# Strided attention on one core: keys and values loaded in thirds, two of them on ScalarE's DMA queue

## The chip, the cores and the metric

The kernel runs on one core of a Trainium2 chip. Its time is the device time of one execution in microseconds. The kernel before was run eight times: the median is 129.92 us, the lowest 129.73, the highest 130.17. One more execution was profiled; it took 129.81 us, and the profile covers a span of 127.7 us of it, from the first to the last instruction.

## What is computed

Q, K and V have the shape (8, 12, 1024, 64) in float32, and `stride` is 64. Every query of a head attends to the same 16 positions of that head, 0, 64, 128 and so on to 960:

```python
attend_positions = np.arange(0, seq, stride)            # 16 of 1024
scores  = einsum('bhqd,bhkd->bhqk', q, k[attend]) / sqrt(64)
weights = exp(scores - max(scores))
weights = weights / (sum(weights) + 1e-10)
result  = einsum('bhqk,bhkd->bhqd', weights, v[attend])
```

So all of Q (25.2 MB) is read and all of the result (25.2 MB) is written, but only one row in 64 of K and of V is used: 96 heads of 16 rows of 64 floats, 0.39 MB of each.

## The kernel before

The 96 heads are worked on in 24 groups of four (`HG = 4`, `NG = 24`); one group is 1 MB of Q and 1 MB of result. Two groups share one "chunk" of 128 key rows (`NC = 12` chunks: 2 groups x 4 heads x 16 positions = 128 partitions). `k_raw` and `v_raw` hold these chunks, 128 partitions by 12 by 64 floats. Each is filled by one DMA before (lines 100 and 102), made of 1,536 rows of 256 bytes.

For a group g the steps are: `load` (the DMA of 1 MB of Q into one of nine `qn` buffers), `cast` to bf16 on POOL (line 211), `transpose` in 32x32 blocks on DVE (215), `scores` on PE (222) with the exponential on ScalarE (233), `sums_mm` and `sums_rec` (242, 251, 255) for the reciprocals of the sums, `outputs` on PE (264), `normalize` on DVE, ScalarE and POOL (277, 278, 282), and `store` (1 MB, from one of eight `out_sb` buffers).

Keys are prepared for eight groups (four chunks) at a time. `key_rows(m)` is four ScalarE instructions (165) that spread the rows of `k_raw`; `keys(m)` is eight small PE matmuls (175) and two ScalarE copies (183) into `k_t`. For the values, one DVE cast turns all of `v_raw` into bf16 (`v_bf`, line 300). `value_rows(n)` takes six chunks at a time: two PE matmuls (192) and two DVE casts out of PSUM (196) into `v_rep`. `values(g)` on POOL (203) builds what `outputs` uses. `key_rows(0)`, `keys(0)` and `value_rows(0)` run ahead of the loop; `key_rows(1)` and `(2)` follow in iterations 1 and 5, `keys(1)` and `(2)` in iterations 2 and 6, and `value_rows(1)` in iteration 3.

The order of the work on each engine is the order of the code. All DMAs are issued by the SP engine, and their order is the code's too: K, the Q block of group 0, V, the Q blocks of groups 1 to 8, and then in each iteration `store(g)` and `load(g + 9)`. Q blocks 0 and 1 are read in 128 rows of 8 KB, the others in 32 rows of 32 KB (line 97). Both `_copy` (line 35 in the profile, for Q and the stores) and `dma_start` (lines 100 and 102) go to the SP queue:

```python
    nc.sync.dma_start(k_raw, _ap_with(K, kv_src))
    load(0)
    nc.sync.dma_start(v_raw, _ap_with(V, kv_src))
    for g in range(1, QBUFS):
        load(g)
```

Of the kernel before, what the change touches and what calls it, by code (L numbers as in the profile page):

```python
# [11 lines left out]
FP32 = mybir.dt.float32  # L12
# [7 lines left out]
def _ap_with(ap: bass.AP, new_ap, extra_offset: int = 0) -> bass.AP:  # L20
    return dataclasses.replace(
        ap, ap=[list(p) for p in new_ap], offset=ap.offset + extra_offset
    )
# [27 lines left out]
def kernel(  # L51
# [8 lines left out]
    nc = tc.nc  # L60

    B, H, S, D = Q.shape
# [3 lines left out]
    P = 128  # L66
    HG = 4
    NG = B * H // HG
    NC = NG // 2
    SD = S * D  # L70
# [14 lines left out]
    psum_s = ctx.enter_context(tc.tile_pool(name="psm", bufs=2, space=bass.MemoryType.PSUM))  # L85
# [4 lines left out]
    k_raw = const.tile([P, NC, D], FP32, name="k_raw")  # L90
    v_raw = const.tile([P, NC, D], FP32, name="v_raw")
    kv_src = [[stride * D, P], [2 * HG * SD, NC], [1, D]]
    qn = {}

    def load(g):
        qn[g] = qn_pool.tile([P, 32 * D], FP32, name="qn", tag="qn")
        n = P if g < 2 else 32
        _copy(nc, qn[g], _ap_with(Q, [[HG * SD // n, n], [1, HG * SD // n]], g * HG * SD))

    nc.sync.dma_start(k_raw, _ap_with(K, kv_src))  # L100
    load(0)
    nc.sync.dma_start(v_raw, _ap_with(V, kv_src))
    for g in range(1, QBUFS):
        load(g)

# [16 lines left out]
    for c in range(2):  # L122
        for a in range(2):
            for e in range(2):
                nc.gpsimd.tensor_copy(
                    out=perm_v[:, c, a, :, e], in_=id_v[:, c, :, a]
# [5 lines left out]
    for i in range(3):  # L132
# [7 lines left out]
        out=slot_i, in0=iota_p, scalar1=4, scalar2=3,  # L140
# [6 lines left out]
        out=s_sel, in0=col4, scalar1=slot_f, scalar2=None, op0=ALU.is_equal  # L147
# [10 lines left out]
    v_bf = const.tile([P, NC, D], BF16, name="v_bf")  # L158
    v_rep = const.tile([P, NC, 2, D], BF16, name="v_rep")


    def key_rows(m):
        kr = k_raw[:, 4 * m : 4 * m + 4].rearrange("p n (q f) -> p n f q", f=2)
        for h in range(4):
            nc.scalar.activation(  # L165
                out=k_m[:, 4 * m : 4 * m + 4, :, h], in_=kr,
                func=AF.Copy, scale=slot_m[:, h : h + 1],
            )

    def keys(m):  # L170
        for u in range(2):
            kp = psum_sc.tile([P, 2, 2, 2, 4 * NK], FP32, name="kp", tag="sc")
            for i in range(2):
                for f in range(2):
                    nc.tensor.matmul(  # L175
                        kp[:, i, :, f],
                        lhsT=k_m[:, 4 * m + 2 * u + i, f].rearrange("p h q -> p (h q)"),
                        rhs=perm_k.rearrange("p c a b k -> p c (a b k)"),
                        start=True, stop=True,
                    )  # L180
            g0 = 8 * m + 4 * u
            dst = k_t[:, g0 : g0 + 4]
            nc.scalar.copy(  # L183
                _ap_with(dst, [dst.ap[0], [KW, 8], [32, 4], [1, NK]], extra_offset=NK),
                kp.rearrange("p i c f (s k) -> p (i c f) s k", s=4),
            )


    def value_rows(n):
        for c in range(2):  # L190
            vp = psum_s.tile([P, NC // 2, D], FP32, name="vp", tag="sm")
            nc.tensor.matmul(
                vp, lhsT=perm_v[:, c].rearrange("p a b e k -> p (a b e k)"),
                rhs=v_bf[:, 6 * n : 6 * n + 6], start=True, stop=True,
            )
            nc.vector.tensor_copy(out=v_rep[:, 6 * n : 6 * n + 6, c], in_=vp)  # L196

    qb, qt, wt, vb, rec, out_sb, o_ps, sm_ps = {}, {}, {}, {}, {}, {}, {}, {}

# [1 line left out]
    def values(g):  # L201
        vb[g] = vb_pool.tile([P, 4, D], BF16, name="vb", tag="vb")
        nc.gpsimd.tensor_tensor(  # L203
            out=vb[g], in0=mask,
            in1=v_rep[:, g // 2, g % 2].unsqueeze(1).to_broadcast([P, 4, D]),
            op=ALU.mult,
        )

    def cast(g):
        qb[g] = qb_pool.tile([P, 32 * D], BF16, name="qb", tag="qb")  # L210
        nc.gpsimd.tensor_copy(out=qb[g], in_=qn[g])  # L211

    def transpose(g):
        qt[g] = qt_pool.tile([P, 32 * D], BF16, name="qt", tag="qt")
        nc.vector.transpose(qt[g].bitcast(I32), qb[g].bitcast(I32))  # L215

    def scores(g):
        sc = psum_sc.tile([P, 512], FP32, name="sc", tag="sc")
        q = qt[g]
        for e in range(2):  # L220
            for f in range(2):
                nc.tensor.matmul(  # L222
                    sc, lhsT=k_t[:, g, f, NK * (1 - e) : NK * (1 - e) + P],
                    rhs=_ap_with(
                        q, [q.ap[0], [D, 8], [16 * D, 2], [2, 32]],
                        extra_offset=8 * D * e + f,
                    ),
                    start=e + f == 0, stop=e + f == 2,
                )
        w = wt[g] = w_bufs[g % 3]  # L230
        for a in range(2):
            wa = w[64 * a : 64 * a + 64]
            nc.scalar.activation(  # L233
                out=_ap_with(wa, [wa.ap[0], [P, 8], [1, 2], [2, 32]], extra_offset=64 * a),
                in_=sc[64 * a : 64 * a + 64].rearrange("p (t x q) -> p t x q", t=8, x=2),
                func=AF.Exp, bias=0.0, scale=scale,
            )

    def sums_mm(g):
        sm = sm_ps[g] = psum_s.tile([P, 8, 32], FP32, name="sm", tag="sm")  # L240
        for q in range(4):
            nc.tensor.matmul(  # L242
                sm[32 * q : 32 * q + 32], lhsT=sel32,
                rhs=wt[g][:, :, 32 * q : 32 * q + 32],
                start=True, stop=True, tile_position=(0, 32 * q),
            )

    def sums_rec(g):
        sm = sm_ps[g]
        smt = rec_pool.tile([P, 8, 32], FP32, name="smt", tag="smt")  # L250
        nc.vector.transpose(  # L251
            smt.rearrange("p i r -> p (i r)"), sm.rearrange("p i r -> p (i r)")
        )
        rec[g] = rec_pool.tile([P, 8, 4], FP32, name="rec", tag="rec")
        nc.vector.reciprocal(rec[g], smt[:, :, 0:4])  # L255


    def outputs(g, c):
        if c == 0:
            out_sb[g] = out_pool.tile([P, 4, 8, D], FP32, name="out_sb", tag="out_sb")  # L260
        ps = psum_o.tile([P, 4, 4, D], FP32, name="o_ps", tag="o")
        o_ps[g, c] = ps
        for i in range(4):
            nc.tensor.matmul(  # L264
                ps[:, i].rearrange("p s d -> p (s d)"), lhsT=wt[g][:, 4 * c + i],
                rhs=vb[g].rearrange("p s d -> p (s d)"),
                start=True, stop=True,
            )

    def normalize(g, c):  # L270
        ps = o_ps[g, c]
        i0 = 4 * c
        n = 4 if c == 0 else 2
        part = lambda k, m: out_sb[g][:, :, k : k + m].rearrange("p s i d -> p i s d")
        fact = lambda k, m: rec[g][:, k : k + m].unsqueeze(3).to_broadcast([P, m, 4, D])
        if n < 4:
            nc.scalar.copy(part(i0 + n, 4 - n), ps[:, n:4])  # L277
        nc.vector.tensor_tensor(  # L278
            out=part(i0, n), in0=ps[:, 0:n], in1=fact(i0, n), op=ALU.mult
        )  # L280
        if n < 4:
            nc.gpsimd.tensor_tensor(  # L282
                out=part(i0 + n, 4 - n), in0=part(i0 + n, 4 - n),
                in1=fact(i0 + n, 4 - n), op=ALU.mult,
            )

    def store(g):
        o = out_sb[g]
        _copy(
            nc,  # L290
            _ap_with(out, [[16 * D, P], [2 * SD, 2], [1, 16 * D]], g * HG * SD),
            _ap_with(o, [o.ap[0], [1, 1], [1, 32 * D]]),
        )
# [3 lines left out]
    cast(1)  # L297
    transpose(0)
    keys(0)
    nc.vector.tensor_copy(out=v_bf, in_=v_raw)  # L300
    scores(0)
    transpose(1)
    value_rows(0)
    values(0)
    values(1)
# [3 lines left out]
    for g in range(NG):  # L309
        if g + 2 < NG:  # L310
            transpose(g + 2)
        if g + 1 < NG:
            scores(g + 1)
        outputs(g, 0)
        outputs(g, 1)
        if g + 1 < NG:
            sums_mm(g + 1)
        if g + 2 < NG:
            values(g + 2)
        if g + 3 < NG:  # L320
            cast(g + 3)
        normalize(g, 0)
        normalize(g, 1)
        if g + 1 < NG:
            sums_rec(g + 1)
        if g in (1, 5):
            key_rows(g // 4 + 1)
        if g in (2, 6):
            keys(g // 4 + 1)
        if g == 3:  # L330
            value_rows(1)
        store(g)
        if g + QBUFS < NG:
            load(g + QBUFS)
# [33 lines left out]
```

The softmax here doesn't subtract the row's maximum and nothing guards it: scores larger than these inputs give would overflow.

## Time and profile before

| | us |
|---|---|
| median of 8 runs | 129.92 |
| the profiled execution | 129.81 |
| its span | 127.7 |
| DVE busy | 95.0 (74%) |
| POOL busy | 90.7 (71%) |
| PE matmul busy | 75.1 (59%) |
| ScalarE busy | 58.8 (46%) |
| last DVE, POOL or PE instruction ends | about 115 |

Busy times are those of one engine's instructions; they overlap each other. The 16 DMA engines of the core move all data between HBM and the on-chip memory, whichever engine issued the DMA, and the profile gives their mean busy share and the bytes moved for any stretch of the span. SPq stands for the instructions that SP uses to issue DMAs. What a DMA issue costs its engine (0.4 to 0.7 us) is not the time of the transfer, which lands many microseconds later.

### The profile page before, as it was taken

Reading aid. Unit: us, or ns where it says so; the run is one execution under the profiler, and the core shown is the slowest. Engines: PE = TensorE matmul, PEld = TensorE weight load, DVE = VectorE, ACT = ScalarE, POOL = GpSimd, SP = SyncE. Lnnn points to the kernel's source line nnn. Section 1 sums busy time; section 2 is a strip of 40 time slices with the busy share of each in tenths; the row PEclk is TensorE's granted clock in tenths of the full one; section 3 lists DMA queues with packets and bytes.
Section 4 is the critical chain, followed back from the end, with each engine's and each line's share of the span. In section 5 each row is a group of like instructions: output and inputs, shape, how many; then the busy total and the mean of one; then the engine's idle time right before and its main releaser. Section 6 shows DMA issues by size and latency. Waiting matters only on the chain. (4 is left out here: it accounts for less than half of the span.)

```text
span 127.7 us, 1413 instructions
## 1 busy us (share of the span) xinstructions
PE 75.1 (59%) x412; PEld 36.0 (28%) x412; DVE 95.0 (74%) x136; ACT 58.8 (46%) x91; POOL 90.7 (71%) x93
## 2 busy tenths in 40 slices
PE   0008399856778787777876396396496485830000
PEld 0003044333444432333333142142142241410000
DVE  6944739999998999999999669678688687890000
ACT  0453444986379775666554443433533642610000
POOL 8983499999969999995965955956956859160000
PEclk9999999999999999999999869959958965798555
DMA  2999989799899999999899899998998999999980
GB/s 62 382 318 470 462 359 493 329 411 472 370 429 444 406 439 459 388 459 447 359 470 452 367 485 390 416 495 372 413 475 365 452 400 426 426 429 421 429 370 33
DMA packets 7911, 51.20 MB, mean 401 GB/s; under 512 B 3872, under 2 KB 3872, under 8 KB 3872
## 3 DMA queue, kind: packets, MB, share of 16 engines
q1 hardware_dynamic: 7904, 51.12, 96.7%
q8 instruction: 3, 0.05, 0.1%
q14 instruction: 4, 0.03, 0.1%
HBM read 25.95 MB, written 25.17 MB: 400 GB/s over the span
## 5 line engine op out<-in xcount | busy, mean ns | idle before, releaser
L211 POOL CAST qb<-qn 128x2048 bf16<-128x2048 f32 x24 | 45.4, 1894 | 16.3 <-DVE out_sb L278 11.0
L233 ACT ACTIVATE w<-sc 64x512 bf16<-64x512 f32 x48 | 35.3, 735 | 45.0 <-PE sc L222 44.4
L278 DVE TENSOR_TENSOR out_sb<-o_ps,rec 128x1024 f32<-128x1024 f32 (+1 forms) x48 | 43.0, 932 | 0.5 <-PE o_ps L264 0.3
L222 PE MATMUL sc<-qt,k_t 128*128 128x512 bf16 x96 | 31.1, 453 | 18.3 <-DVE qt L215 17.3
L215 DVE STREAM_TRANSPOSE qt<-qb 128x1024 int32<-128x1024 int32 x24 | 29.2, 1218 | 15.3 <-POOL qb L211 15.2
L264 PE MATMUL o_ps<-vb,w 128*128 128x256 bf16 x192 | 31.3, 304 | 1.0 <-DVE out_sb L278 0.4
L282 POOL TENSOR_TENSOR out_sb<-out_sb,rec 128x512 f32<-128x512 f32 x24 | 25.0, 1044 | 5.3 <-ACT out_sb L277 5.3
L264 PEld LDWEIGHTS <-w 128*128 128x128 bf16 x192 | 19.7, 109 | 17.6 <-DVE out_sb L278 9.1
L222 PEld LDWEIGHTS <-k_t 128*128 128x128 bf16 x96 | 9.5, 104 | 30.9 <-issue 23.1
L242 PE MATMUL sm<-w,sel 128*32 128x256 bf16 x96 | 12.9, 298 | 8.1 <-ACT w L233 5.9
L203 POOL TENSOR_TENSOR vb<-mask,v_rep 128x256 bf16<-128x256 bf16 x24 | 16.0, 670 | 1.8 <-DVE v_rep L196 1.8
L277 ACT COPY out_sb<-o_ps 128x512 f32<-128x512 f32 x24 | 14.1, 586 | 2.6 <-POOL out_sb L282 1.5
L255 DVE RECIPROCAL rec<-smt 128x32 f32<-128x32 f32 x24 | 8.5, 353 | 2.7 <-DVE smt L251 0.5
L251 DVE STREAM_TRANSPOSE smt<-sm 128x256 f32<-128x256 f32 x24 | 10.3, 428 | 0.0
L242 PEld LDWEIGHTS <-sel 128*32 128x32 bf16 x96 | 4.8, 94 | 17.8 <-issue 15.2
L175 PE MATMUL kp<-perm_k,k_m 128*128 128x128 bf16 x24 | 2.3, 250 | 9.3 <-ACT k_m L165 9.3
L165 ACT ACTIVATE k_m<-k_raw,slot_m 128x256 bf16<-128x256 f32 x12 | 5.3, 519 | 1.4 <-DVE slot_m L153 1.4
L175 PEld LDWEIGHTS <-k_m 128*128 128x128 bf16 x24 | 1.7, 112 | 9.5 <-ACT k_m L165 9.3
L136 POOL MEMSET k_t<- 128x4608 bf16 x1 | 3.9, 3946 | 0.0
L183 ACT CAST k_t<-kp 128x512 bf16<-128x512 f32 x6 | 3.2, 589 | 0.9 <-PE kp L175 0.7
L165 ACT ACT_TABLE_LOAD x1 | 1.3, 1283 | 4.8 <-DMA k_raw<-in_K_dram 4.8
L146 DVE TENSOR_SCALAR s_sel<-col,slot_f 128x4 bf16<-128x4 int16 x1 | 3.2, 3157 | 0.1
(22 smaller groups left out, 10.9 us busy)
## 6 DMA issues: line engine op xcount, KB each, us to landing
qn<-in_Q_dram SPq DMA_DIRECT2D x24, 1024.0 KB, 17.7
out_dram<-out_sb SPq DMA_DIRECT2D x24, 1024.0 KB, 17.5
k_raw<-in_K_dram SPq DMA_DIRECT2D x1, 384.0 KB, 4.0
v_raw<-in_V_dram SPq DMA_DIRECT2D x1, 384.0 KB, 7.0
```

The costliest lines, as they stand in the source:

```text
L203: nc.gpsimd.tensor_tensor(out=vb[g], in0=mask, in1=v_rep[:, g // 2, g % 2].unsqueeze(1).to_broadcast([P, 4, D]), op=ALU.mult,)
L211: nc.gpsimd.tensor_copy(out=qb[g], in_=qn[g])
L215: nc.vector.transpose(qt[g].bitcast(I32), qb[g].bitcast(I32))
L222: nc.tensor.matmul(sc, lhsT=k_t[:, g, f, NK * (1 - e) : NK * (1 - e) + P], rhs=_ap_with(q, [q.ap[0], [D, 8], [16 * D, 2], [2, 32]], extra_ ...
L233: nc.scalar.activation(out=_ap_with(wa, [wa.ap[0], [P, 8], [1, 2], [2, 32]], extra_offset=64 * a), in_=sc[64 * a : 64 * a + 64].rearrange( ...
L242: nc.tensor.matmul(sm[32 * q : 32 * q + 32], lhsT=sel32, rhs=wt[g][:, :, 32 * q : 32 * q + 32], start=True, stop=True, tile_position=(0, 3 ...
L251: nc.vector.transpose(smt.rearrange("p i r -> p (i r)"), sm.rearrange("p i r -> p (i r)"))
L255: nc.vector.reciprocal(rec[g], smt[:, :, 0:4])
L264: nc.tensor.matmul(ps[:, i].rearrange("p s d -> p (s d)"), lhsT=wt[g][:, 4 * c + i], rhs=vb[g].rearrange("p s d -> p (s d)"), start=True, ...
L277: nc.scalar.copy(part(i0 + n, 4 - n), ps[:, n:4])
L278: nc.vector.tensor_tensor(out=part(i0, n), in0=ps[:, 0:n], in1=fact(i0, n), op=ALU.mult)
L282: nc.gpsimd.tensor_tensor(out=part(i0 + n, 4 - n), in0=part(i0 + n, 4 - n), in1=fact(i0 + n, 4 - n), op=ALU.mult,)
```

## The change

The two DMAs of K and V become six, each of four chunks (eight groups, 512 rows of 256 bytes, 128 KB). The first third of K is issued on SP ahead of Q block 0, and the first third of V behind it. The other four are issued on the ScalarE queue, ahead of everything else that ScalarE does; in the code they stand ahead of the loads of Q blocks 1 to 8.

`value_rows` now takes four chunks, like `keys`, and casts its own part of `v_raw` first, so the single cast of line 300 goes. In the loop, `key_rows(1)` and `(2)` move to iterations 4 and 12, and `keys` and `value_rows` of the same eight groups to iterations 5 and 13.

```diff
-    nc.sync.dma_start(k_raw, _ap_with(K, kv_src))
+    def load_kv(queue, tile_, src, m):
+        queue.dma_start(
+            tile_[:, 4 * m : 4 * m + 4],
+            _ap_with(src, kv_src[:1] + [[2 * HG * SD, 4]] + kv_src[2:], 8 * m * HG * SD),
+        )
+
+    load_kv(nc.sync, k_raw, K, 0)
     load(0)
-    nc.sync.dma_start(v_raw, _ap_with(V, kv_src))
+    load_kv(nc.sync, v_raw, V, 0)
+    for m in range(1, 3):
+        load_kv(nc.scalar, k_raw, K, m)
+        load_kv(nc.scalar, v_raw, V, m)
     for g in range(1, QBUFS):
         load(g)
...
-    def value_rows(n):
+    def value_rows(m):
+        n0 = 4 * m
+        nc.vector.tensor_copy(out=v_bf[:, n0 : n0 + 4], in_=v_raw[:, n0 : n0 + 4])
         for c in range(2):
-            vp = psum_s.tile([P, NC // 2, D], FP32, name="vp", tag="sm")
+            vp = psum_s.tile([P, 4, D], FP32, name="vp", tag="sm")
             nc.tensor.matmul(
                 vp, lhsT=perm_v[:, c].rearrange("p a b e k -> p (a b e k)"),
-                rhs=v_bf[:, 6 * n : 6 * n + 6], start=True, stop=True,
-            )
-            nc.vector.tensor_copy(out=v_rep[:, 6 * n : 6 * n + 6, c], in_=vp)
+                rhs=v_bf[:, n0 : n0 + 4], start=True, stop=True,
+            )
+            nc.vector.tensor_copy(out=v_rep[:, n0 : n0 + 4, c], in_=vp)
...
     keys(0)
-    nc.vector.tensor_copy(out=v_bf, in_=v_raw)
     scores(0)
...
-        if g in (1, 5):
-            key_rows(g // 4 + 1)
-        if g in (2, 6):
-            keys(g // 4 + 1)
-        if g == 3:
-            value_rows(1)
+        if g in (4, 12):
+            key_rows(g // 8 + 1)
+        if g in (5, 13):
+            keys(g // 8 + 1)
+            value_rows(g // 8 + 1)
```

## The prediction

> **What bounds the kernel now.** I read the page first, its busy row and its slices of the DMA engines, then the busy times by stretch, then SP's own waits.
>
> ```profile
> span 127.7 us, 1413 instructions
> ...
> DMA  2999989799899999999899899998998999999980
> GB/s 62 382 318 470 462 359 493 329 411 472 370 429 444 406 439 459 388 459 447 359 470 452 367 485 390 416 495 372 413 475 365 452 400 426 426 429 421 429 370 33
> DMA packets 7911, 51.20 MB, mean 401 GB/s; under 512 B 3872, under 2 KB 3872, under 8 KB 3872
> ...
> q1 hardware_dynamic: 7904, 51.12, 96.7%
> ```
>
> No compute engine is above 74%, but the one DMA queue holds the 16 DMA engines for 96.7% of the span. The single digits of 7 and 8 are records that fall into neighbouring slices; longer stretches show it (columns: stretch, length, busy time of PE, weight loads, DVE, ScalarE, POOL with counts, clock, DMA share, GB/s):
>
> ```profile
> 2.00:4.00 2.00, 0.00 (x0) 0.00 (x0) 1.69 (x6) 0.00 (x0) 2.00 (x10) 1.00 0.91 212
> 4.00:8.00 4.00, 0.00 (x0) 0.00 (x0) 3.59 (x5) 1.80 (x3) 3.71 (x2) 1.00 1.10 353
> 8.00:24.00 16.00, 11.56 (x53) 5.08 (x54) 10.14 (x14) 8.21 (x15) 11.98 (x10) 1.00 1.03 425
> 24.00:46.00 22.00, 16.23 (x110) 8.89 (x109) 20.98 (x32) 16.74 (x29) 20.70 (x19) 1.00 1.02 426
> 46.00:114.00 68.00, 47.28 (x250) 22.05 (x249) 56.64 (x80) 32.05 (x48) 50.24 (x45) 0.87 1.00 423
> 114.00:124.00 10.00, 0.00 (x0) 0.00 (x0) 0.96 (x2) 0.00 (x0) 0.67 (x1) 0.64 1.00 421
> ```
>
> From about 4 to 124 us the share is 1.00 and the rate 421 to 426 GB/s: the DMA engines never stand idle. 51.2 MB at 425 GB/s is 120.5 us, and what is left of the span is some 2 us ahead of the first byte, the slow rows of K and V, and the tail. SP's waits say the same from the other side:
>
> ```profile
> SPq L35 <- DMA out_dram<-out_sb: 17.9, 9, 2.0
> SPq L35 <- DMA qn<-in_Q_dram: 15.5, 9, 1.7
> ...
> SPq L363 <- DMA out_dram<-out_sb: 10.6, 1, 10.6
> ```
>
> These are from 46 us on. SP stands waiting for earlier transfers to land, and at the end the program waits 10.6 us for stores that were issued long before. That 10.6 us is the cover of all compute: the last store is issued at 115.0. The transfers' own list for the same stretch shows how deep the queue is:
>
> ```profile
> out_dram<-out_sb SPq DMA_DIRECT2D x17, 1024.0 KB, 19.5
> qn<-in_Q_dram SPq DMA_DIRECT2D x8, 1024.0 KB, 19.6
> ```
>
> SP issues one Q block every 4.9 us (50.26, 55.16, 60.05 us in its timeline) and one store between; a transfer lands 19.6 us after its issue, which is four such pairs. So a transfer is issued when the eighth before it has landed: eight are in flight, no more. This matters below.
>
> **The change part by part.**
>
> *Bytes and pieces.* The bytes stay, and so do the 3,072 rows of 256 bytes. (The page counts 3,872 packets under 512 B; the other 800 are 16 closing packets for each of 50 transfers.) Four more transfers make 64 more closing packets. Priced like rows of V (1,536 in 1.57 us, below: 1.02 ns each over 16 engines) they are 0.07 us on the path that sets the end. Below, 0.
>
> *The price of a small row beside large ones.* Before, K and V pass alone in the one queue. While V passes (7.3 to 8.8 us, 40 slices) the rate is:
>
> ```profile
> GB/s 287 259 280 259 259 266 266 232 273 239 239 225 253 218 239 437 212 410 826 553 546 89 307 82 505 458 232 225 0 0 218 218 0 1092 218 437 0 218 0 437
> ```
>
> The first 15 slices average 253 GB/s, against 425 for Q and stores. I take 250: 0.393 MB of V is 1.57 us. The two thirds that move, 0.524 MB, cost 2.10 us today. No row shows rows of 256 bytes in a second queue beside large ones. From below: if they filled gaps and cost only their bytes at 425, 1.23 us, a gain of 0.87. From above: K's start is the slowest passage of such rows in the trace, 135 GB/s from 2 to 3 us in the stretches of 1 us; at that rate they cost 3.9 us, a loss of 1.8. I take today's price, so 0: the nearest row is V itself, and its flat rate right behind a landed Q block, with all its commands issued five microseconds earlier, looks like a fixed price per row inside the DMA engine and not like waiting that another queue could fill.
>
> [...]
>
> *SP.* Two issues remain of K and V as before (0.43 and 0.59 us); nothing is removed or added on SP. What moves is the count of eight. Before, the first eight are K, Q0, V, Q1 to Q5, and only Q6 to Q8 wait, for K, Q0 and V, which have landed by about 9 us. After, the first eight are the six small transfers, Q0 and Q1, if ScalarE's transfers count in the same eight. Then Q2 to Q8 each wait for one of the six or for Q0. Behind a waiting Q block on SP stand the other Q blocks and store(0), and `cast` waits for those. If the two queues share the DMA engines about evenly, all small rows (0.786 MB at 250 GB/s, 3.1 us) and at most as much time of Q have passed by about 2 + 7 = 9 us, as V has today, while four Q blocks (2.5 us each) are still to come: the wait costs nothing. The other outcome is rival 1.
>
> *ScalarE.* Four DMA issues of 0.43 to 0.73 us (SP's rows for K and Q0) are 1.7 to 2.9 us ahead of its table load. ScalarE is idle there until 4.81 us, waiting for K, and `key_rows(0)` then waits for `slot_m` from DVE until 7.48:
>
> ```profile
> 4.81 1.28 ACT L165 ACT_TABLE_LOAD   x1 [4.81 <-DMA k_raw<-in_K_dram]
> 7.48 1.76 ACT L165 ACTIVATE k_m<-k_raw,slot_m 128x256 bf16<-128x256 f32 x4 [1.39 <-DVE slot_m L153]
> ```
>
> Cost 0. The same line shows that K's earlier landing gains nothing either: DVE's `slot_m` is later.
>
> *Start of the loop.* Ahead of Q1 there were 0.786 MB of small rows; after, between 0.262 MB (a starved ScalarE queue) and all of it. Q1 lands 0 to 2.1 us sooner, and the cast of group 1, which starts at 11.60 after 2.2 us of waiting for it, may start at 9.5. This gain goes into the 10.6 us of waiting at the end and shortens nothing: the last store's bytes come after all the others however early they are ready.
>
> *Compute.* DVE: one cast of 0.519 us becomes three of 0.17 (a third) to 0.28 (the 128x256 copy of `mask`): 0 to +0.33. Four casts out of PSUM of 0.524 become six of 0.35 (two thirds) to 0.43 (line 251, 128x256 out of PSUM): 0 to +0.5. PE: four matmuls of 0.426 become six of 0.298 (line 242, also 256 columns), +0.1, and two weight loads of 0.12. ScalarE's 12 + 6 instructions stay. In iterations 5 and 13 PE waits for DVE's new cast; the one like it today cost PE 1.2 us (line 192), so 2.4 in all. `key_rows` and `keys` run two iterations ahead of `scores(8)` and `scores(16)`; that is some 7 us at 3.5 us an iteration early on. All this is at most 3.6 us against the cover of 10.6, so 0; without cover it would be those 3.6.
>
> *Sum.* 129.81 for the profiled execution + 0.07 = 129.9 us, 0.02 under the median of the runs.
>
> **The rivals.**
>
> 1. *The count of eight empties SP's queue (slower).* If the DMA engines give the ScalarE queue one row for each 8 KB of Q, or less, its 128 rows per DMA engine need 128 turns. SP's first thirds of K and V have 64 rows per engine and a Q block 8 such pieces, so 128 turns end only with Q7's last byte, at about 22 to 25 us, and Q8, waiting for the last of the four, is not issued until then. With SP's queue empty the rest passes at once, Q8 is issued, and its first byte comes as long after its issue as K's: issued 0.74, first bytes at about 2.1, so 1.4 us. With up to 0.4 for the landing and the wait on SP, the DMA engines idle 1.2 to 1.8 us, and nothing gives that back: 131.1 to 131.7 us. It decides once a ScalarE transfer lands later than about 1.8 us before the last byte of the Q block ahead of the one that waits for it. For it: the depth of eight. Against it: an even share ends the small rows by 9 us.
> [...]
> 2. *Switching costs (slower).* Rows of 256 bytes between large ones fall to the rate of K's first microsecond: up to +1.8, 131.6; middle 130.8. For it: nothing in the trace but that slow start. Against it: V's flat rate.
> 3. *Small rows fill gaps (faster).* -0.35 to -0.87: 129.0 to 129.5. For it: K and V run at 60% of the full rate alone. Against: the same flat rate.
> 4. *It does not do what it says*: ScalarE's transfers are issued as early as SP's and pass beside the first third, so Q0 and Q1 land no sooner. Same time; part of the forecast.
>
> **How the numbers follow.** About 0.2% (0.26 us) can be told from no change. Forecast, with rival 4: 0.48, between 129.5 and 130.3; of it 0.08 faster, 0.34 the same, 0.06 slower. Rival 1: 0.20, slower. Rival 2: 0.12, slower. Rival 3: 0.20, faster. So faster 0.28, same 0.34, slower 0.38. The range runs from the far end of rival 3, 128.9, to that of rivals 1 and 2, 131.7; the forecast's own range is 129.5 to 130.3.
>
> **What would show it.** A DMA share of 1.00 from 4 us to the tail, with a higher rate in the first 10 us, is the forecast or rival 3; a hole in the DMA slices near 20 to 25 us, with SP waiting for `k_raw` or `v_raw`, is rival 1; a share of 1.00 at a rate well under 425 for longer than 4 us is rival 2. The cast of group 1 should start between 9.5 and 11.6 us, and the wait of line 363 at the end should stay near 10 us. I would be wrong throughout if the wait at the end shrank to nothing, for then compute would set the end.

## The result and the profile after

The changed kernel takes 133.53 us (median of 11 runs) against 129.91 us for the kernel before on the same chips: a ratio of 1.0266, 95% interval 1.0253 to 1.0279. It is 3.6 us slower. The ratio leaves out two of the eleven runs, 134.86 and 135.04 us, which fell in a slower state; the median of the other nine is 133.37. The profiled execution took 133.78 us, 4.0 more than the profiled one of the kernel before.

The page of the changed kernel, the span, the slices of the DMA engines and the queues:

```profile
span 132.0 us, 1426 instructions
...
DMA  5999994998998998998998998999999999999970
GB/s 102 332 395 475 381 421 118 397 328 290 489 412 380 472 432 372 472 442 370 454 447 377 457 449 375 457 442 382 449 449 377 449 395 434 427 417 427 432 320 17
DMA packets 7975, 51.20 MB, mean 388 GB/s; under 512 B 3936, under 2 KB 3936, under 8 KB 3936
...
q1 hardware_dynamic: 5856, 50.60, 92.9%
q10 hardware_dynamic: 2112, 0.52, 1.8%
```

The bytes are the same, and the packets are 64 more, as worked out. What is new is the 4 in the seventh slice, from 19.8 to 23.1 us, with 118 GB/s: the DMA engines stand idle there (a share of 0.00 from 21 to 22 us). ScalarE's queue is q10, with 2,048 rows and 64 closing packets.

The same stretches in both kernels, first the kernel before, then the changed one (the last two columns are the DMA share and GB/s):

```profile
12.00:20.00 8.00, 5.82 (x25) 2.25 (x24) 4.49 (x7) 3.52 (x5) 6.19 (x6) 1.00 1.02 430
20.00:24.00 4.00, 3.52 (x19) 1.63 (x18) 3.96 (x6) 2.36 (x4) 4.00 (x4) 1.00 0.94 393
28.00:36.00 8.00, 5.70 (x36) 3.09 (x36) 7.79 (x12) 4.70 (x8) 6.79 (x6) 1.00 1.09 453
36.00:110.00 74.00, 52.75 (x289) 25.17 (x288) 62.44 (x89) 38.24 (x59) 58.73 (x51) 0.89 1.00 422
```

```profile
12.00:20.00 8.00, 7.14 (x29) 2.79 (x28) 4.61 (x8) 4.11 (x7) 5.58 (x6) 1.00 0.96 398
20.00:24.00 4.00, 3.25 (x20) 1.47 (x19) 3.97 (x6) 2.32 (x4) 4.00 (x4) 1.00 0.55 162
28.00:36.00 8.00, 6.27 (x39) 3.09 (x40) 7.79 (x12) 6.41 (x11) 8.00 (x8) 1.00 1.06 379
36.00:110.00 74.00, 51.00 (x284) 24.67 (x282) 61.05 (x88) 38.11 (x59) 54.85 (x47) 0.86 1.00 423
```

Two losses stand out. From 20 to 24 us, 231 GB/s less for 4 us is 0.92 MB, which is 2.2 us at 425 GB/s: a hole, at a share of 0.55. From 28 to 36 us, 74 GB/s less for 8 us is 0.59 MB, 1.4 us: here the share is 1.06, so the engines are busy but slow. After 36 us the rates are the same.

Such rows are rough. They count a piece where it starts, and sixteen pieces of 32 KB are 0.52 MB, or 1.2 us; so the first rows differ too, by 0.6 us. If the bytes of every record in the two traces are spread over the record's own time instead, the changed kernel is 0.2 us ahead at 20 us, 2.5 behind at 28, and 3.7 behind at 36 and at 110 us. So the hole is 2.2 us by the rows and 2.7 by the records, the slow stretch 1.4 and 1.2, and up to 110 us nothing else is lost.

SP's waits name the hole:

```profile
SPq L35 <- DMA k_raw<-in_K_dram: 12.8, 2, 12.2
SPq L35 <- DMA v_raw<-in_V_dram: 3.2, 1, 3.2
...
SPq L372 <- DMA out_dram<-out_sb: 10.4, 3, 5.6
```

SP, ready to issue a Q block, waited 12.2 us for one transfer of K to land. Before, it never waited for K or V. The wait at the end is still 10.4 us (10.6 before), so compute still does not set the end. When K landed is in the list of its tile:

```profile
DMA to landing us min/median/max: 2.7/2.9/19.4
```

The slowest is the last third, issued at 1.85 us on ScalarE: it landed at 21.3 us. In SP's timeline the next three Q blocks, 6 to 8, are issued from 21.31 us on.

### The profile page after: what moved, and what is told of

Same layout as the page of the kernel before. It is cut to its first block, busy times and chain, and to the rows that moved or that the text cites. A ratio compares the mean times of both kernels' runs of the same rounds, so it can differ in the third digit from the quotient of the medians.

```text
span 132.0 us, 1426 instructions
## 1 busy us (share of the span) xinstructions
PE 76.6 (58%) x414; PEld 36.5 (28%) x414; DVE 98.6 (75%) x140; ACT 58.9 (45%) x91; POOL 90.8 (69%) x93
## 4 chain that ended last, share of the span: by engine, by line
DMA 45%; DVE 15%; POOL 14%; issue 8%; PE 5%; ACT 2%; DVEq 1%; SPq 0%; POOLq 0%
DMA qn<-in_Q_dram 45%; POOL qb L222 10%; DVE out_sb L289 7%; DVE s_sel L155 4%; PE sc L233 3%; POOL out_sb L293 2%; POOL vb L214 1%; ACT k_m L174 1%; PE o_ps L275 1%; DVE qt L226 1%; DVE w L143 1%; DVE k_t L139 1%; PE kp L184 0%; DVEq L372 0%; ACT k_t L192 0%
## 5 line engine op out<-in xcount | busy, mean ns | idle before, releaser
L275 PE MATMUL o_ps<-vb,w 128*128 128x256 bf16 x192 | 32.3, 309 | 1.3 <-DVE out_sb L289 0.6
L203 PE MATMUL vp<-v_bf,perm_v 128*128 128x256 bf16 x6 | 1.8, 396 | 7.0 <-DVE v_bf L200 7.0
L155 DVE TENSOR_SCALAR s_sel<-col,slot_f 128x4 bf16<-128x4 int16 x1 | 5.0, 4982 | 0.1
```

Of the source, the lines that this page charges most:

```text
L155: nc.vector.tensor_scalar(out=s_sel, in0=col4, scalar1=slot_f, scalar2=None, op0=ALU.is_equal)
L275: nc.tensor.matmul(ps[:, i].rearrange("p s d -> p (s d)"), lhsT=wt[g][:, 4 * c + i], rhs=vb[g].rearrange("p s d -> p (s d)"), start=True, ...
```

## The experiments

**e1: one queue.** All six transfers on SP, in the order of the changed kernel.

```diff
-        load_kv(nc.scalar, k_raw, K, m)
-        load_kv(nc.scalar, v_raw, V, m)
+        load_kv(nc.sync, k_raw, K, m)
+        load_kv(nc.sync, v_raw, V, m)
```

> The changed kernel with all six transfers of K and V on SP, in the same order ahead of Q blocks 1 to 8. Theory A (the rows on ScalarE's queue are starved by the Q blocks, and SP waits for them through the count of eight, so that the DMA engines run empty at 21 us): the hole goes, 129.7 to 130.2 us. Theory B (what costs is the later start of the loop, ScalarE's key rows at 9.3 in place of 7.5 us, and the moved work): still 133 to 134 us. If the slow Q block at 28 to 32 us of the changed kernel follows from the hole, it goes as well; if it does not, 131.0 to 131.5.

Measured: 131.23 us, ratio 1.0105 (1.0068 to 1.0143). Most of the loss goes with the second queue, but 1.4 us stay. That lies in the 131.0 to 131.5 set for a slow block that does not follow from the hole, but by luck: there is no such block (442 GB/s from 28 to 32 us). By the records, e1 is 1.0 us behind the kernel before at 12 us and 1.1 at 110, so it loses at the start, which neither theory named. e12 looks for that.

**e2: the moved work alone.** The changed kernel's `value_rows` and its iterations, with these loads:

```diff
-    load_kv(nc.sync, k_raw, K, 0)
+    nc.sync.dma_start(k_raw, _ap_with(K, kv_src))
     load(0)
-    load_kv(nc.sync, v_raw, V, 0)
-    for m in range(1, 3):
-        load_kv(nc.scalar, k_raw, K, m)
-        load_kv(nc.scalar, v_raw, V, m)
+    nc.sync.dma_start(v_raw, _ap_with(V, kv_src))
```

> The kernel before with the compute part of the change alone: value rows by four chunks, keys and values prepared in iterations 4, 5, 12 and 13, the loads as before. Theory A: 129.7 to 130.2 us, since 10.6 us of waiting at the end cover it. Theory B: some or all of the 3.6 us, above 131.

Measured: 129.70 us, ratio 0.9988 (0.9976 to 1.0001). The work that moved costs nothing. The other part of theory B, the later key rows, is not in this kernel; e5 below has it and is not slower, and e4 is as slow as the changed kernel with key rows at 7.5 us. So theory B falls.

**e3: the last thirds on POOL.**

```diff
-    for m in range(1, 3):
-        load_kv(nc.scalar, k_raw, K, m)
-        load_kv(nc.scalar, v_raw, V, m)
+    load_kv(nc.scalar, k_raw, K, 1)
+    load_kv(nc.scalar, v_raw, V, 1)
...
     nc.gpsimd.memset(k_t[:, 8:NG], 0.0)
+    load_kv(nc.gpsimd, k_raw, K, 2)
+    load_kv(nc.gpsimd, v_raw, V, 2)
```

> The changed kernel with the last thirds of K and V issued by POOL behind its start-up work, whose transfers are not in the count of eight that SP waits on; the second thirds stay on ScalarE. Still a second queue with small rows beside the Q blocks. Theory A: the last thirds land late, after 25 us, but no Q block waits for them, no hole, 129.7 to 130.5 us. Rival C (a second queue of small rows slows the DMA engines by itself, whoever waits): 131.5 to 134 us.

Measured: 129.78 us, ratio 1.0005 (0.9978 to 1.0033). The same two stretches, in this kernel:

```profile
20.00:24.00 4.00, 3.22 (x20) 1.36 (x17) 3.97 (x6) 2.06 (x3) 4.00 (x4) 1.00 0.96 401
28.00:36.00 8.00, 6.27 (x39) 3.10 (x40) 7.79 (x12) 6.39 (x11) 8.00 (x8) 1.00 1.07 452
```

No hole, no slow stretch, and the time of before: rows of K and V beside Q blocks did not slow the DMA engines by more than the interval's 0.3%, so rival C falls. One expectation missed: the last thirds did not land after 25 us but some 7.6 and 9.8 us after their issue at 7.1 and 8.0, at 14.7 and 17.8. The queues of this kernel from 8 to 16 us say why:

```profile
q1 hardware_dynamic: 206, 3.24, 102.3%
q0 software_dynamic: 79, 0.26, 9.3%
```

POOL's 0.26 MB went in 79 packets; 64 of 4 KB make up the bytes, 16 rows in a packet. So by a count of packets, which e4 bears out below, they had 64 to pass in place of 1,024. SP's waits in this kernel name K not at all and V once, for 2.5 us, and no hole came of it.

**e4: smaller pieces of Q.** This tells a share by packets from a share by time.

```diff
-        n = P if g < 2 else 32
+        n = P
```

> The changed kernel with every Q block read in 128 pieces of 8 KB (blocks 2 and up have 32 pieces of 32 KB in the changed kernel). Theory A with one row of ScalarE's queue for each piece of Q: the rows come four times as often once blocks 0 and 1 are through; the last third of K lands at about 16 to 17 us in place of 21.5, the last third of V at 23 to 24, and the hole moves from 21 us to 23 or 24 us, because Q block 7 waits for that V; the time stays within 0.7 us of the changed kernel's. If the two queues share by time or by bytes, both landings and the hole stay where they are, near 21.5 us.

Measured: 134.02 us, ratio 1.0329 (1.0282 to 1.0376). The queues from 12 to 20 us, first the changed kernel, then e4:

```profile
q1 hardware_dynamic: 146, 3.15, 94.0%
q10 hardware_dynamic: 161, 0.04, 2.3%
```

```profile
q1 hardware_dynamic: 434, 3.16, 96.0%
q10 hardware_dynamic: 426, 0.11, 6.2%
```

This is the cause in two pairs of lines. While both queues had work, they passed about one packet for one packet: 146 against 161 where Q came in pieces of 32 KB, 434 against 426 where it came in pieces of 8 KB. A packet on ScalarE's queue was one row of 256 bytes. So 3.15 MB of Q let 0.04 MB of K and V through. ScalarE's queue was not slow by itself: in the changed kernel, from 20 to 21 us, as SP's queue ran out of data, it passed 498 packets in one microsecond.

```profile
q10 hardware_dynamic: 498, 0.12, 54.9%
```

In e4 the last third of K lands earlier and that of V sets the hole; the list of K's tile, SP's waits and the stretches:

```profile
DMA to landing us min/median/max: 2.7/2.9/14.0
```

```profile
SPq L35 <- DMA v_raw<-in_V_dram: 11.8, 2, 7.8
...
SPq L35 <- DMA k_raw<-in_K_dram: 6.5, 2, 5.9
```

```profile
20.00:24.00 4.00, 3.16 (x22) 1.40 (x21) 3.97 (x6) 2.70 (x5) 4.00 (x5) 1.00 0.85 341
24.00:28.00 4.00, 2.80 (x17) 1.32 (x17) 3.90 (x7) 2.06 (x4) 4.00 (x4) 1.00 0.66 209
```

K's last third landed at 15.9 us (issued 1.9) in place of 21.3, and V's at 24.1 (issued 2.6, 21.5 to landing), and the hole moved from 20 to 24 into 24 to 28 us, as the count of packets had it. A share by time or bytes falls.

**e7, e8, e9, e11: the slow stretch.** What is slow from 28 to 32 us in the changed kernel is the reading of Q block 8, the last block in SP's queue ahead of store 0. Four kernels ask what that depends on: eight Q buffers in place of nine; the kernel before with 1 MB more to read; the load ahead of the store in each iteration; and the kernel before with six Q buffers, which empties the one queue without any ScalarE transfer.

```diff
-    QBUFS = 9
+    QBUFS = 8
```

> The changed kernel with eight Q buffers in place of nine, so that block 7 is the last ahead of store 0. Theory A: the same hole at 21 us, and a time within 0.7 us of the changed kernel's. The slow block: if it is the last Q block ahead of the first store, it is now block 7, at about 26 to 29 us; if it is whatever is read between 28.5 and 32 us, block 7 runs at the usual 2.5 us and store 0 passes there at its usual 2.5 to 2.8 us, with at most a slow block 8 behind it.

```diff
     nc.sync.dma_start(v_raw, _ap_with(V, kv_src))
+    extra = const.tile([P, 32 * D], FP32, name="extra")
+    _copy(nc, extra, _ap_with(Q, [[HG * SD // 32, 32], [1, HG * SD // 32]], 23 * HG * SD))
```

> The kernel before with one more block of 1 MB read from Q into a tile that nothing uses, behind V. No hole; block 8 is read at 28.7 to 31.2 us, as late as in the changed kernel. If the slow block comes from the hole: 2.45 us more than before, 132.2 to 132.6. If reads are slow at that time in any kernel: 133.4 or more, with block 8 taking 3.5 us.

```diff
-        store(g)
         if g + QBUFS < NG:
             load(g + QBUFS)
+        store(g)
```

> The changed kernel with load(g + 9) ahead of store(g) in each iteration, so that Q block 9 and not block 8 is the last one ahead of store 0. The hole at 21 us stays. If the slow block is the last Q block ahead of the first store, it is now block 9 (3.5 us between its landing and the one before, block 8 at the usual 2.5). If it is block 8, or simply the third block after the hole, block 8 stays slow. Time within 0.7 us of the changed kernel's in either case.

```diff
-    QBUFS = 9
+    QBUFS = 6
```

> The kernel before with six Q buffers in place of nine: one queue, no starved rows. Blocks 0 to 5 have landed at 21.7 us, and the next transfer on SP, store 0, is issued at about 21.9. Theory A (an empty queue costs its own length and nothing gives it back): a hole of 1.5 to 1.8 us at 21.7 to 23.5 us and 131.3 to 132 us, if later stores keep up. If slow reads follow any hole, another 1 us or more on top, and Q pieces of 1.5 to 2.2 us in place of 1.22 behind the hole. If a hole is made good later: 129.9.

| kernel | us | ratio, interval |
|---|---|---|
| e7, eight buffers | 133.44 | 1.0266 (1.0242 to 1.0291) |
| e8, one more MB | 132.43 | 1.0189 (1.0165 to 1.0214) |
| e9, load first (two runs) | 133.78 | 1.0300 (1.0246 to 1.0354) |
| e11, before with six buffers | 134.00 | 1.0315 (1.0288 to 1.0343) |

The stretch of the slow block in the changed kernel, in e7 and in e9, each with a stretch beside it:

```profile
24.00:28.30 4.30, 3.38 (x22) 1.59 (x21) 4.20 (x7) 2.37 (x4) 4.30 (x5) 1.00 1.12 434
28.30:32.10 3.80, 2.94 (x19) 1.35 (x17) 3.70 (x7) 2.26 (x4) 3.80 (x4) 1.00 0.76 222
```

```profile
25.80:29.50 3.70, 3.03 (x18) 1.36 (x19) 3.60 (x7) 2.63 (x4) 3.70 (x5) 1.00 0.79 224
29.50:36.00 6.50, 4.78 (x27) 2.25 (x27) 6.40 (x9) 4.93 (x10) 6.50 (x6) 1.00 1.01 425
```

```profile
28.00:30.50 2.50, 1.96 (x14) 0.98 (x13) 2.40 (x5) 2.06 (x3) 2.50 (x4) 1.00 1.12 419
30.50:34.50 4.00, 2.82 (x17) 1.33 (x17) 3.90 (x7) 2.48 (x5) 4.00 (x4) 1.00 0.83 213
```

With one block fewer ahead of store 0 the slow stretch comes 2.5 us sooner, with one block more 2.2 us later. So in these three it is neither a time nor a block number: it is the last Q block ahead of the first store.

The stretches begin a little behind the block's first pieces, so their GB/s are too low; the time of a piece is surer. Block 8 in the queue's own line, in the kernel before (25.5 to 27.5 us), in e8 (28 to 30) and in the changed kernel (28 to 31):

```profile
q1 hardware_dynamic: 48, 1.05, 124.8%
q1 hardware_dynamic: 48, 1.05, 124.8%
q1 hardware_dynamic: 48, 1.05, 124.7%
```

Of the 48 packets 32 are pieces and 16 closing packets. 124.8% of 16 engines for 2 us are 39.9 us, 1.25 us for a piece; 124.7% for 3 us are 59.9 us, 1.87 us for a piece. Worked out in the same way, it is 1.89 us in e7 and 2.06 in e9; in e1 it is 1.3. e8 shows that the slow block needs the hole: block 8 is read as late as in the changed kernel, and the time is 132.43, 2.4 us over before's 130.03 in that set, just what 1 MB costs at 425 GB/s (2.5). And e11 shows that it needs neither a second queue nor that place in the order:

```profile
20.00:24.00 4.00, 3.42 (x18) 1.70 (x19) 3.97 (x7) 2.31 (x5) 4.00 (x4) 1.00 0.19 80
24.00:28.00 4.00, 3.02 (x24) 1.58 (x22) 3.90 (x6) 3.80 (x8) 4.00 (x4) 1.00 1.01 330
28.00:36.00 8.00, 5.38 (x35) 2.88 (x34) 7.79 (x13) 4.58 (x8) 5.29 (x6) 1.00 1.00 388
```

Against before's 393, 393 and 453 that is 2.9, 0.6 and 1.2 us; the run is 4.1 us slower, so the length of the hole is not given back. The hole, expected at 1.5 to 1.8 us, is longer. What is slow behind it here is the last third of store 0 (48 pieces of 8 KB from 25 to 26.5 us, 0.53 us each in place of 0.31) and then Q block 6 (1.64 us a piece), which is behind the first store. So "the last block ahead of the first store" does not hold in general. Why slow pieces follow a hole was not settled. By the records, pieces of Q and of stores took 1.5 to 2.0 us longer (over 16 engines, against 1.24 us for 32 KB and 0.31 for 8 KB) between the hole and 35 us in all five kernels with a hole, and at most 0.15 us longer in the others. In the changed kernel that is 1.6 us, of which 0.4 are in block 6 and counted with the hole above.

**e12: the 1.4 us of e1.** All on SP, K's thirds ahead of Q block 0 and V's behind it.

```diff
-    load_kv(nc.sync, k_raw, K, 0)
+    for m in range(3):
+        load_kv(nc.sync, k_raw, K, m)
     load(0)
-    load_kv(nc.sync, v_raw, V, 0)
-    for m in range(1, 3):
-        load_kv(nc.scalar, k_raw, K, m)
-        load_kv(nc.scalar, v_raw, V, m)
+    for m in range(3):
+        load_kv(nc.sync, v_raw, V, m)
```

> The changed kernel with all six transfers on SP, but the three of K ahead of Q block 0 and the three of V behind it: the byte order of the kernel before. If the one-queue kernel of e1 was 1.3 us slow because a first third of 32 rows per DMA engine is over before Q block 0's first bytes can come (its first pieces took 0.9 to 1.6 us), it is back at 129.7 to 130.3 us here. If six transfers in place of two cost by themselves, 131 or more.

Measured: 130.36 us, ratio 1.0037 (1.0024 to 1.0050). Going back to the byte order of before gives back 0.9 of the 1.4 us; about 0.5 stay with the six commands. That the short first third leaves a gap ahead of Q block 0 is not shown: by the records of the profiled executions e12 is 0.9 us behind the kernel before at 12 us, nearly as far as e1. Where e12 gets its time back stays open.

**e5, e6, e10: second queues without a wait.** e5 and e10 are the same kernel, the changed one with the last thirds on SP behind Q block 8; e6 is the kernel before with V on ScalarE's queue.

```diff
-    for m in range(1, 3):
-        load_kv(nc.scalar, k_raw, K, m)
-        load_kv(nc.scalar, v_raw, V, m)
+    load_kv(nc.scalar, k_raw, K, 1)
+    load_kv(nc.scalar, v_raw, V, 1)
     for g in range(1, QBUFS):
         load(g)
+    load_kv(nc.sync, k_raw, K, 2)
+    load_kv(nc.sync, v_raw, V, 2)
```

> The changed kernel with the last thirds of K and V on SP behind Q block 8; the second thirds stay on ScalarE, and Q2 and Q4, which wait for them, find them landed by 9 us. Theory A: no hole, 129.5 to 130.1 us. If the slow Q block of the changed kernel at 28 to 32 us is due to something other than the hole, 130.8 or more.

```diff
-    nc.sync.dma_start(v_raw, _ap_with(V, kv_src))
+    nc.scalar.dma_start(v_raw, _ap_with(V, kv_src))
```

> The kernel before with one word changed: V, whole, is issued on ScalarE's queue. Its rows pass beside those of K, before Q block 0 begins, so nothing starves: both land by about 6 us and no Q block waits. Theory A: no hole, 129.3 to 130.0 us; the two queues together fill the first two microseconds better (0.2 to 0.4 us). Rival C (a second queue costs by itself): over 130.5.

> The kernel of e5 once more, with more rounds, since its interval reached from 0.995 to 1.0005 of the kernel before. Theory A (the 16 DMA engines set the time, and the order of the bytes does not): 0.997 to 1.000, at most 0.4 us better.

Measured: e5 129.48 us, 0.9976 (0.9947 to 1.0005); e10 129.52 us, 0.9986 (0.9965 to 1.0006); e6 129.94 us, 0.9999 (0.9975 to 1.0023). All three keep small rows on ScalarE's queue, and none is slower. In e6 the rows were expected to land by about 6 us, ahead of most of Q; the time agrees with that, and when they landed is not shown. The first microseconds were not filled better: 177 GB/s from 2 to 4 us, before 212. e5 is half of the change without its fault; if it is faster than before, it is by some 0.3 us, which these runs do not set apart from nothing.

## Why the prediction was wrong, point by point

- **What bounds the kernel: right.** 422 and 423 GB/s from 36 to 110 us in both kernels, and in e8 1 MB more costs 2.4 us.
- **Bytes and the price of a row: right.** 64 more packets, and rows of K and V beside Q cost about what they cost alone: 161 packets at 2.3% of 16 engines for 8 us are 18 ns each, where 16 (1.02 times 16) were reckoned, and e3 and e5 are within 0.3% of before. Neither rival 2 nor rival 3 came. The near end of rival 3, 0.35 us of gain, is shown by no run; with small rows on a second queue and no hole, e3 and e5 came out at 1.0005 and 0.9976 of before.
- **SP: this step failed.** It was allowed that ScalarE's transfers count among the eight, so that Q2 to Q8 wait for the small ones. Then came "if the two queues share the DMA engines about evenly", and by it "the wait costs nothing". The queues shared by packets, 161 of them with 0.04 MB on ScalarE's queue against 146 with 3.15 MB on SP's from 12 to 20 us, and the last third of K landed at 21.3 us, not by 9. SP waited 12.2 us for it, the wait put at nothing, and the queue ran empty: 2.2 to 2.7 us for the hole and 1.2 to 1.4 for the slow pieces behind it.
- **Rival 1 had the mechanism, at 0.20, and was priced too low** at 1.2 to 1.8 us. Three things differ. It reckoned with pieces of 8 KB and so had Q8 wait for the last transfer, at 22 to 25 us; with pieces of 32 KB it was the third of K that came late, at 21.3, and e4 with pieces of 8 KB has the hole at 24. The hole is worth 2.2 us by the rows and 2.7 by the records, not 1.4 + 0.4: SP's queue was already running out while the last rows passed (20 to 21 us, 0.12 MB). And the slow block behind it, 1.2 to 1.4 us, was in no part of the sum. These two are what 131.7, the far end of rival 1, lacked.
- **ScalarE: cost right, a detail wrong.** Its four issues took 0.49, 0.57, 0.76 and 0.53 us, 2.35 in all, and hid. But `key_rows(0)` starts at 9.32 us, not at 7.48, because DVE's `slot_m` is later (below). e5 has that delay too and is not slower.
- **Start of the loop: right.** The cast of group 1 starts at 10.89, within 9.5 to 11.6.
- **Compute: right that it is hidden** (e2, and 10.4 us of waiting at the end), low in size: DVE is busy 3.6 us longer (95.0 to 98.6), 1.8 of them in `s_sel`, and one of the three casts of V took 1.34 us in place of the 0.17 to 0.28 reckoned.

## What to carry to other kernels

In this kernel, which its DMA engines bound (a share of 1.00 at 422 GB/s from 36 to 110 us before), the empty queue cost the most: 2.2 to 2.7 us, and 1.2 to 1.4 in slow pieces behind it. The order of the bytes and the number of transfers cost less (all six transfers on one queue: 1.4 us in e1, 0.5 in e12). So the question that a second queue raised here, and the first to ask of another kernel, is not its load but who waits for its transfers, and how many packets, not bytes, they are against the packets of the other queue: 128 rows of 256 bytes for each DMA engine, beside Q in pieces of 8 and 32 KB, took about 20 us, and SP, with eight transfers in flight and no more (a landing 19.6 us after its issue, and 2.45 us for each transfer), waited 12.2 us for one third of them to land. Two ways out had times within 0.3% of before: nothing that feeds the first queue waits for the late ones (e3 at 1.0005, e5 at 0.9976), or they are issued so that, by the author's estimate, they are over before the large pieces start (e6 at 0.9999).

## What the runs showed of the hardware that was not expected

- A hole in the DMA stream cost more than its length: 1.5 to 2.0 us more in slow pieces behind it, by the records of the five kernels that had one. The cause is open.
- POOL's queue packed 16 rows of 256 bytes into a packet (64 packets of 4 KB for 0.26 MB in e3) where ScalarE's made each row one (2,048 packets for 2,048 rows in the changed kernel).
- A DVE instruction on 4 elements a partition, `s_sel`, took 3.16 us before and 4.98 us after. The timeline of the changed kernel, DVE and then POOL:

```profile
4.02 4.98 DVE L155 TENSOR_SCALAR s_sel<-col,slot_f 128x4 bf16<-128x4 int16 x1
```

```profile
7.08 1.90 POOL L222 CAST qb<-qn 128x2048 bf16<-128x2048 f32 x1
```

It ends at 9.00, within 0.02 us of POOL's cast at 8.98. Before, it ended at 7.17, just after POOL's memset (3.20 + 3.95 = 7.15), in the 0.29 us in which POOL waited for Q block 0. In the changed kernel that block lands sooner, and the cast follows the memset with no gap. The instructions behind it show the same in other kernels. In e5 the copy into `sel` took 1.79 us in place of 0.17 and ended at 8.98 (7.19 + 1.79), POOL's cast at 8.96 (7.07 + 1.89); in e9 the cast into `slot_m` took 1.88 in place of 0.16 and ended at 9.17 (7.29 + 1.88), POOL's cast at 9.14 (7.25 + 1.89). Where POOL's cast came later, at 8.21 in e4 and 9.24 in e12, none of the four instructions behind `s_sel` took over 0.28 us. Why one of them lasts as long as POOL's instruction is not shown.
